# Ten pairs of the mixer's input columns (attention and gate strips) as seven half-size block products each, with their weight sums made in the first FFN

## The chip, the cores and the metric

The kernel runs on one core of one Trainium2 chip. The metric is device time in microseconds (us), as the median of several executions. Five engines work beside each other, each in its own program order: TensorE (PE: matmuls), VectorE (DVE: elementwise), ScalarE (ACT: copies and functions), GpSimd (POOL), and SyncE (SP), which here issues nearly all DMA transfers. An instruction that waits holds up everything behind it on its engine.

## What is computed

One layer of a decoder on 1024 tokens with a model width of 1024. `norm` is a root-mean-square norm with a gain; the two FFNs, the mixer and its three branches are all float32.

```python
f1 = swiglu(norm(h), ffn1_w_in, ffn1_w_out)          # width 2816
h  = h + 0.5 * norm(f1)
u  = norm(h)
p_rwkv, p_swa, q_mem, gate_logits = split(u @ w_in)  # 1792 + 768 + 512 + 3072 columns
y_a = rwkv7_mix(p_rwkv, ...)                         # a recurrence over the 1024 tokens, 8 heads of 64
y_b = sliding_window_gqa_sinks(p_swa, ...)           # 8 query heads, 2 key heads, window 128
y_c = memory_cross_attention(q_mem, mem_n, mem_w_kv) # 4 heads, 256 memory tokens
g_a, g_b, g_c = split(sigmoid(gate_logits + gate_b))
merged = g_a * (y_a @ w_branch[0]) + g_b * (y_b @ w_branch[1]) + g_c * (y_c @ w_branch[2])
h  = h + norm(merged @ w_out)
f2 = swiglu(norm(h), ffn2_w_in, ffn2_w_out)
h  = h + 0.5 * norm(f2)
```

The change touches how part of `u @ w_in` is computed. `w_in` has 6144 columns, held as 48 strips of 128 columns: strips 0 to 13 feed the recurrence, 14 to 19 the window attention, 20 to 23 the memory attention, 24 to 47 the 24 gates (gate g is strip 24 + g).

## The kernel before

**Layout.** Everything stands feature by token: a tile has 128 features as partitions and 512 tokens (`TH`), so the 1024 tokens are two halves, h = 0 and 1, and the model width is eight blocks k. A product of float32 precision is made of three matmuls (`mm3`, L361; lines 364, 365, 366): every factor x is split into a rounded part hi (ACT copies it) and the rest lo (DVE subtracts), and hi·hi, hi·lo and lo·hi are summed in PSUM. One strip of 128 output columns for both halves of the tokens (`project`, L368) is thus 8 x 2 x 3 = 48 matmuls of 128x512.

**Weights.** `plan` (L238) writes down the order in which all weights are used. A raw half strip of 128x512 is loaded by SP into one of five `w_raw` buffers (`raw`, L274, issue at L279), and `operand` (L284) makes `w_hi` on ACT (L288) and `w_lo` on DVE (L290). Eight operands are kept ahead of their use (`OPS`). `take` hands out the next one.

**Block products.** The FFNs already use a scheme with seven half-size products in place of eight: the two strips and the two halves of the tokens are the 2 x 2 blocks of a product, four sums of weight blocks and four of activation blocks ("forms" t1 to t4) are made first, seven products of 4 x 3 = 12 matmuls each follow (84 in place of 96 for two strips), and their results are added on DVE. In the first FFN a pair j of strips runs so, 22 in all (`ffn_in_pair`, L700). While the pairs 9 to 19 run, DVE also makes weight sums for the FFN's second matrix (`sums_loads`, L637, `sums_made`, L650): per step four loads of 128x512 by SP (L641), four DVE operations (L655 to L658), four stores (L660).

**The mixer** (`mixer`, L1584). `rwkv_prep` makes the recurrence's inputs, with DVE nearly full. `rwkv_invert` (L1120) inverts 128 triangular 64x64 matrices on DVE alone: 62 steps of two operations (L1129, L1130), each on the result of the one before, `x` being loaded from `ab_d` (L1124) and stored to `inv_d` (L1132). Meanwhile PE runs the attention strips (`att_block`, tile `pq`) and the first 8 gates (`gate_block`, `GATES_FIRST`, tile `pgate`). Then comes `rwkv_chain` (L1135): 16 steps, each a series of small matmuls on PE and small operations on DVE, ACT and POOL that wait for each other. The scheduler lays the matmuls of the gates 8 and 9 (up to `GATES_EARLY`) into the holes of the chain. After it, `rwkv_finish` and the two attentions run as blocks of 128 tokens: 8 memory blocks, then 8 window blocks (`attention`, L1501). Between a block's scores, its softmax on DVE and ACT, its transposes (`mptr`, `ptr`) and its values, `fill` (L1342) puts a number of other matmuls on PE, given by the list of lumps. These fills come from `filling` (L1317): gates 10 to 23, then the branch products. Each finished gate or branch strip also starts one step of the weight sums for the second FFN (`unit`, L670; tile `gin`, L655).

**Order.** A scheduler orders every engine's queue from program order and priorities; some engines' orders are fixed by `issue_after` and `high_priority`. SP's queue is one: a store that waits for its data stands in the way of the loads behind it.

**PSUM** has eight banks: four for tiles of the large products (`po px py pr pgate pq pb pw`), four for all others.

Of the kernel before, what the change touches and what calls it, by code (L numbers as in the profile page):

```python
# [47 lines left out]
GATES_EARLY = 10  # L48
LUMPS = (30, 54)
GATES_FIRST = 8  # L50
# [173 lines left out]
class Builder:  # L224
# [3 lines left out]

    def out_strip(self, f, n, q):
        a = OUT_FORMS[n][1]  # L230
        return self.sum_d[f][SUMS.index(a), q] if a in SUMS else self.io[f + "_out"][a, q]
# [6 lines left out]
    def plan(self):  # L238
        io, seq = self.io, []
        for f in ("ffn1", "ffn2"):  # L240
# [3 lines left out]
            if f == "ffn1":  # L244
# [4 lines left out]
                seq += [("win", j) for j in ATT_BLOCKS]  # L249
                seq += [("win", 24 + g) for g in range(24)]  # L250
# [386 lines left out]
    def sums_loads(self, f, q, a):  # L637

        with self.tc.issue_after(self.loaded.ins):
            for n, t in enumerate(a):  # L640
                self.nc.sync.dma_start(t, self.io[f + "_out"][n, q])  # L641
        return a

    def sums_tiles(self, pool):
        return [pool.tile([P, KH, P], F32, tag="ws", name="ws", bufs=4) for _ in range(4)]
# [4 lines left out]
    def sums_made(self, f, q, a, behind):  # L650
# [8 lines left out]
        for n, t in zip(SUMS, (a22, a11, a21, a12)):  # L659
            nc.sync.dma_start(self.sum_d[f][SUMS.index(n), q], t)  # L660
# [474 lines left out]
    def rwkv_chain(self, pool, pk_d, inv_d, y):  # L1135
# [65 lines left out]
        n = load(0)  # L1201
        G.memset(n["sv"][lo, 0], 0.0)
# [40 lines left out]
        return lambda: out(NC_ - 1, before)  # L1243

    def rwkv_finish(self, pool, y, bonus_d, ya_d):
# [42 lines left out]
        for i, (p, cols) in enumerate(halves):  # L1288
# [11 lines left out]
            if i % 2:  # L1300
                self.fill(10, end)

# [281 lines left out]
    def mixer(self, u, cp, close_raws, att_d, gate_d, km_d, vm_d):  # L1584
# [7 lines left out]
        self.sg = cp.tile([P, T], F32, name="sg")  # L1592
        with tc.tile_pool(reuse_waits="tile", name="prep", bufs=8) as pool:
            self.rwkv_prep(u, pool, pk_d, ab_d, bonus_d, att_d)
        close_raws()
        with tc.tile_pool(reuse_waits="tile", name="gates", bufs=2) as gp:
            with tc.tile_pool(reuse_waits="tile", name="inv", bufs=1) as pool:
                self.rwkv_invert(pool, ab_d, inv_d)
            for f in ATT_BLOCKS[ATT_FIRST:]:
                self.att_block(f, u, att_d, lambda: gp.tile([P, T], F32, tag="gate", name="att", bufs=2))  # L1600
            for g in range(GATES_FIRST):
                self.gate_block(g, u, gp, gate_d)
            with tc.tile_pool(reuse_waits="tile", name="chain", bufs=2) as pool:
                y = pool.tile([P, NPAIR, T], F32, name="y", bufs=1)
                last = self.rwkv_chain(pool, pk_d, inv_d, y)
                for g in range(GATES_FIRST, GATES_EARLY):
# [6 lines left out]
            with tc.tile_pool(reuse_waits="tile", name="att", bufs=1) as ap, tc.tile_pool(name="attw", bufs=2) as pool:  # L1613
# [54 lines left out]
                self.attention(blocks, [42, 34] + [LUMPS[0]] * (nb - 2) + [LUMPS[1]] * nb, {0: [tables], 1: [keys], 2: [load_values], 4: [turn_values]})  # L1668
# [46 lines left out]
    def build(self):  # L1715
        nc, tc, io = self.nc, self.tc, self.io
        with contextlib.ExitStack() as outer, tc.tile_pool(reuse_waits="tile", name="consts", bufs=1) as cp, \
             tc.tile_pool(reuse_waits="tile", name="w", bufs=1) as self.wpool, \
             tc.tile_pool(reuse_waits="tile", name="pmm", bufs=8, space=bass.MemoryType.PSUM) as self.pmm:
            self.sum_d = {f: tc.dram_tile([len(SUMS), KP, P, KH, P], F32, name=f + "_sum_d") for f in ("ffn1", "ffn2")}  # L1720
            self.plan()
# [25 lines left out]
            form_d = tc.dram_tile([len(OUT_FORMS), KP, P, TH], F32, name="form_d")  # L1747
            first_d = tc.dram_tile([max(FIRST.values()), 2, P, TH], F32, name="first_d")
# [127 lines left out]
```

## Time and profile before

| what | us |
|---|---|
| three executions | 2263.18, 2260.92, 2261.9 |
| median | 2261.9 |
| profiled execution, first to last instruction (span) | 2260.2 |
| PE busy, 11876 matmul instructions | 2236.6 |
| DVE busy, 2719 instructions | 1652.0 |
| ACT busy, 1880 instructions | 1000.2 |
| POOL busy, 114 instructions | 58.1 |

The profiled execution has no time of its own beside its span; the span lies 1.7 us below the median. "Busy" counts the time in which an engine executes something. The stages, in us from the start of the span: the pairs of the first FFN with the weight sums run to about 430, its second matrix and the norms to about 720, `rwkv_prep` to about 900, the inverse from 908 to 1029, the chain from 1048 to about 1150, the attentions from about 1180 to about 1450. Rows called "windows" give, for a stretch A:B, its length, then each engine's busy time with its count of instructions (PE, PE's weight loads, DVE, ACT, POOL), the granted PE clock, the share of time in which the 16 DMA engines were busy, and what they moved in GB/s.

### The profile page before, as it was taken

How to read it: one execution, taken by the hardware profiler on the slowest of the kernel's cores; microseconds unless marked ns; L12 is line 12 of the kernel's file. 1: busy time of each engine (PE TensorE's matmuls, PEld its weight loads, DVE VectorE, ACT ScalarE, POOL GpSimd, SP SyncE). 2: the span in 40 equal slices, each digit the busy share in tenths (PEclk: the TensorE clock that was granted, in tenths of full speed). 3: DMA queues.
4: the chain of work that ended last, by engine and by line, in shares of the span. 5: the costliest groups of instructions: out<-in, count | busy, mean ns of one | idle time of the engine just before them, and what ended most of it. 6: DMA issues, size and time to landing. Idle time of an engine off the chain costs nothing.

```text
span 2260.2 us, 33447 instructions
## 1 busy us (share of the span) xinstructions
PE 2236.6 (99%) x11876; PEld 1840.4 (81%) x11876; DVE 1652.0 (73%) x2719; ACT 1000.2 (44%) x1880; POOL 58.1 (3%) x114
## 2 busy tenths in 40 slices
PE   8999999999999999999999999999999999999998
PEld 6888888888888788888888887788888888888887
DVE  6987777666698886995666576684898885656576
ACT  6533333454556653223454445334663233345451
POOL 0000000000000000001320000000000000000000
PEclk9999999999999999999999999999999999999999
DMA  8465666686654467325438885654565542347663
GB/s 291 157 210 168 215 212 208 214 276 207 191 173 149 117 143 183 118 93 194 144 113 289 266 278 186 209 177 136 173 214 188 189 168 90 116 165 250 204 196 122
DMA packets 280775, 417.66 MB, mean 185 GB/s; under 512 B 82304, under 2 KB 104320, under 8 KB 280352
## 3 DMA queue, kind: packets, MB, share of 16 engines
q1 hardware_dynamic: 272832, 400.26, 55.3%
q10 hardware_dynamic: 7776, 15.28, 2.0%
q8 instruction: 93, 1.52, 0.3%
q14 instruction: 74, 0.61, 0.1%
HBM read 284.89 MB, written 129.50 MB: 183 GB/s over the span
## 4 chain that ended last, share of the span: by engine, by line
PE 93%; DVE 4%; DMA 1%; ACT 1%; issue 1%; SPq 0%; DVEq 0%; ACTq 0%
PE px L365 7%; PE px L364 7%; PE px L366 7%; PE po L365 6%; PE po L366 6%; PE po L364 6%; PE pgate L364 4%; PE pgate L366 4%; PE pgate L365 4%; PE pz L365 3%; PE pz L364 3%; PE pz L366 3%; PE pb L364 2%; PE pb L365 2%; PE pb L366 2%; PE pr L364 2%
## 5 line engine op out<-in xcount | busy, mean ns | idle before, releaser
L288 ACT CAST w_hi<-w_raw 128x512 fp32r<-128x512 f32 x594 | 367.5, 620 | 734.5 <-PE px L365 159.7
L290 DVE TENSOR_TENSOR w_lo<-w_raw,w_hi 128x512 fp32r<-128x512 f32 x594 | 407.6, 687 | 196.0 <-ACT w_hi L288 175.2
L366 PE MATMUL po<-u,w_lo 128*128 128x512 f32 (+1 forms) x476 | 180.9, 380 | 0.0
L364 PE MATMUL po<-u,w_hi 128*128 128x512 f32 (+1 forms) x476 | 180.9, 380 | 0.0
L365 PE MATMUL po<-u,w_hi 128*128 128x512 f32 (+1 forms) x476 | 180.9, 380 | 0.0
L364 PE MATMUL pgate<-u,w_hi 128*128 128x512 f32 x384 | 153.2, 399 | 0.0
L366 PE MATMUL pgate<-u,w_lo 128*128 128x512 f32 x384 | 151.4, 394 | 0.0
L365 PE MATMUL pgate<-u,w_hi 128*128 128x512 f32 x384 | 149.8, 390 | 0.0
L365 PE MATMUL px<-f,w_hi 128*128 128x512 f32 x352 | 137.2, 390 | 1.0 <-DVE f L473 1.0
L364 PE MATMUL px<-u,w_hi 128*128 128x512 f32 x352 | 137.0, 389 | 0.8 <-DVE km L1442 0.8
L364 PE MATMUL px<-f,w_hi 128*128 128x512 f32 x352 | 137.1, 389 | 0.1
L366 PE MATMUL px<-u,w_lo 128*128 128x512 f32 x352 | 137.0, 389 | 0.0
L366 PE MATMUL px<-f,w_lo 128*128 128x512 f32 x352 | 137.0, 389 | 0.0
L365 PE MATMUL pz<-u,w_hi 128*128 128x512 f32 x352 | 137.0, 389 | 0.0
L365 PE MATMUL px<-u,w_hi 128*128 128x512 f32 x352 | 136.9, 389 | 0.0
L364 PE MATMUL pz<-u,w_hi 128*128 128x512 f32 x352 | 136.9, 389 | 0.0
L366 PE MATMUL pz<-u,w_lo 128*128 128x512 f32 x352 | 136.9, 389 | 0.0
L473 DVE TENSOR_TENSOR u<-hid,u 128x512 fp32r<-128x512 f32 x114 | 78.3, 690 | 46.5 <-ACT u L472 43.5
L364 PEld LDWEIGHTS po<-u,w_hi 128*128 128x128 f32 x476 | 89.5, 188 | 17.1
L365 PEld LDWEIGHTS po<-u,w_hi 128*128 128x128 f32 x476 | 89.5, 188 | 17.1
L366 PEld LDWEIGHTS po<-u,w_lo 128*128 128x128 f32 x476 | 89.5, 188 | 16.8
L472 ACT CAST u<-hid 128x512 fp32r<-128x512 f32 x114 | 70.7, 620 | 64.3 <-DMA hid<-form_d 55.7
(401 smaller groups left out, 5097.4 us busy)
## 6 DMA issues: line engine op xcount, KB each, us to landing
w_raw<-in_ffn_in SPq DMA_DIRECT2D x220, 256.0 KB
hid<-form_d SPq DMA_DIRECT2D x154, 256.0 KB
w_raw<-in_win SPq DMA_DIRECT2D x112, 256.0 KB
form_d<-g SPq DMA_DIRECT2D x88, 256.0 KB
w_raw<-ffn_sum_d SPq DMA_DIRECT2D x88, 256.0 KB
form_d<-h SPq DMA_DIRECT2D x66, 256.0 KB
w_raw<-in_ffn_out SPq DMA_DIRECT2D x66, 256.0 KB
gate_d<-gate SPq DMA_DIRECT2D x24, 512.0 KB
```

The source lines that it names most:

```text
L288: self.nc.scalar.copy(hi, x)
L290: self.split_last = self.nc.vector.tensor_tensor(lo, x, hi.bitcast(F32), ALU.subtract)
L364: mm(out, wh, xh, start=first, stop=False, **kw)
L365: mm(out, wh, xl, start=False, stop=False, **kw)
L366: self.last_mm = mm(out, wl, xh, start=False, stop=last, **kw)
L472: self.nc.scalar.copy(hi, x)
L473: self.nc.vector.tensor_tensor(lo, x, hi.bitcast(F32), ALU.subtract)
```

## The change

Ten pairs of strips are computed with the seven products: the three attention pairs (16, 17), (20, 21), (22, 23) and the seven pairs of the gates 0 to 13. Their weight sums (four for each pair) are made during the first FFN: a second set of four DVE operations, four loads and four stores stands beside the set already there in the steps j = 9 to 16, and the pairs 8 and 9 of the ten have theirs in j = 20 and 21. The sums go to `win_sum_d` and come back as weights. `pre_norm` now writes the normed activations in place and stores them to `xn_d`; `mix_forms` loads them in pieces (`part`, five buffers), makes the four sums per k and splits them. `win_pair` runs the seven products and three DVE additions. The second halves of strips 14 and 15 and gate 14 come first, then the ten pairs beside `rwkv_invert`; the chain has the gates 15 and 16 beside it, and `filling` the gates 17 to 23, so the lumps between the attention blocks are smaller.

```diff
-GATES_EARLY = 10
-LUMPS = (30, 54)
-GATES_FIRST = 8
+GATES_EARLY = 17
+LUMPS = (18, 36)
+GATES_FIRST = 14
+ATT_PAIRS = ((16, 17), (20, 21), (22, 23))
+WIN_PAIRS = ATT_PAIRS + tuple((24 + g, 25 + g) for g in range(0, GATES_FIRST, 2))
+SECOND_UNITS = 8
...
@@ plan
-                seq += [("win", j) for j in ATT_BLOCKS]
-                seq += [("win", 24 + g) for g in range(24)]
+                seq += [("win", j) for j in FILL]
+                seq += [("win", 24 + GATES_FIRST)]
+                seq += [("win_out", (i, n)) for i in range(len(WIN_PAIRS)) for n in range(7)]
+                seq += [("win", 24 + g) for g in range(GATES_FIRST + 1, 24)]
...
@@ pre_norm
-            t = pool.tile([P, TH], F32, tag="un", name="un", bufs=2)[:, : hi - lo]
-            self.nc.vector.scalar_tensor_tensor(t, xs[k], self.vec(gname, k), rs, ALU.mult, ALU.mult)
-            self.split(t, *(y[:, lo:hi] for y in u[k][h]))
+            self.nc.vector.scalar_tensor_tensor(xs[k], xs[k], self.vec(gname, k), rs, ALU.mult, ALU.mult)
+            self.split(xs[k], *(y[:, lo:hi] for y in u[k][h]))
+            self.nc.sync.dma_start(self.xn_d[:, k, h * TH + lo : h * TH + hi], xs[k])
...
@@ ffn_in
-                if f == "ffn1" and FIRST[f] <= j < FIRST[f] + KP:
-                    self.sums_made(f, j - FIRST[f], self.sums_loads(f, j - FIRST[f], self.sums_tiles(pool)), made)
+                if f == "ffn1" and j >= FIRST[f]:
+                    i = j - FIRST[f]
+                    if i < SECOND_UNITS:
+                        self.sums_made("win", i, self.sums_loads("win", i, self.sums_tiles(pool, f"sq{TH}")), self.up)
+                    what = (f, i) if i < KP else ("win", i - KP + SECOND_UNITS)
+                    if what[0] == f or what[1] < len(WIN_PAIRS):
+                        self.sums_made(*what, self.sums_loads(*what, self.sums_tiles(pool)), made)
...
+    def mix_forms(self, u, pool, parts):
...
+        with self.tc.high_priority(offset=self.lead):
+            for k in range(KH):
+                x12, x22, x11, x21 = (parts() for _ in range(4))
+                for t, j, h in ((x12, k, 1), (x22, k + KH, 1), (x11, k, 0), (x21, k + KH, 0)):
+                    self.nc.sync.dma_start(t, self.xn_d[:, j, h * TH : (h + 1) * TH])
+                V.tensor_tensor(x22, x22, x12, ALU.subtract)
+                V.tensor_tensor(x12, x12, x11, ALU.subtract)
+                V.tensor_tensor(x11, x22, x11, ALU.add)
+                V.tensor_tensor(x21, x21, x11, ALU.subtract)
+                for n, x in (("t2", x11), ("t1", x12), ("t3", x22), ("t4", x21)):
+                    self.split(x, *fs[n][k])
+        return fs
+
+    def win_pair(self, i, fs, parts, out, att_d, gate_d):
...
+        part(0, "b11", px, True)
+        x = kept(px)
+        part(1, "b21", py, True, True)
+        made(0, first, 0, py, x)
+        part(2, "t2", px)
+        u1 = kept(px)
+        part(3, "t1", pz, True)
+        z = kept(pz)
+        part(4, "t3", px)
+        made(1, second, 1, px, z)
+        part(5, "b22", pz, False, True)
+        made(0, first, 1, pz, u1)
+        part(6, "t4", px, False, True)
+        made(1, second, 0, px)
...
@@ mixer
-                self.rwkv_invert(pool, ab_d, inv_d)
-            for f in ATT_BLOCKS[ATT_FIRST:]:
-                self.att_block(f, u, att_d, lambda: gp.tile([P, T], F32, tag="gate", name="att", bufs=2))
-            for g in range(GATES_FIRST):
-                self.gate_block(g, u, gp, gate_d)
+                fs = self.mix_forms(u, forms, parts)
+                for f in FILL[ATT_FIRST:]:
+                    self.att_block(f, u, att_d, out)
+                self.gate_block(GATES_FIRST, u, gp, gate_d)
+                self.rwkv_invert(pool, ab_d, inv_d)
+                for i in range(len(WIN_PAIRS)):
+                    self.win_pair(i, fs, parts, out, att_d, gate_d)
...
-                self.attention(blocks, [42, 34] + [LUMPS[0]] * (nb - 2) + [LUMPS[1]] * nb, {0: [tables], 1: [keys], 2: [load_values], 4: [turn_values]})
+                self.attention(blocks, [26, 20] + [LUMPS[0]] * (nb - 2) + [LUMPS[1]] * nb, {0: [tables], 1: [keys], 2: [load_values], 3: [turn_values]})
```

**Where it moves instructions.** On DVE, at the start of the inverse (`itmp<-inv` and `inv<-inv,itmp` are its two operations per step), there stood before:

```order
L290 TENSOR_TENSOR w_lo<-w_raw,w_hi 128x512 x7
L1129 TENSOR_TENSOR itmp<-inv 128x62
L1130 TENSOR_TENSOR inv<-inv,itmp 128x62
L1129 TENSOR_TENSOR itmp<-inv 128x122
L1130 TENSOR_TENSOR inv<-inv,itmp 128x2x61
L1129 TENSOR_TENSOR itmp<-inv 128x180
L1130 TENSOR_TENSOR inv<-inv,itmp 128x3x60
```

At the same place in the changed kernel, the sums of the activation blocks (`part<-part`) and their splits (`mix_form`) for k = 1 stand between the first steps; those for k = 2 and 3 follow in the same way:

```order
L1147 TENSOR_TENSOR itmp<-inv 128x62
L302 TENSOR_TENSOR w_lo<-w_raw,w_hi 128x512
L1148 TENSOR_TENSOR inv<-inv,itmp 128x62
L1336 TENSOR_TENSOR part<-part 128x512
L302 TENSOR_TENSOR w_lo<-w_raw,w_hi 128x512
L1337 TENSOR_TENSOR part<-part 128x512
L1147 TENSOR_TENSOR itmp<-inv 128x122
L1338 TENSOR_TENSOR part<-part 128x512
L1148 TENSOR_TENSOR inv<-inv,itmp 128x2x61
L1339 TENSOR_TENSOR part<-part 128x512
L302 TENSOR_TENSOR w_lo<-w_raw,w_hi 128x512
L485 TENSOR_TENSOR mix_form<-part,mix_form 128x512
```

So 24 operations on the forms for k = 1 to 3 share DVE with the inverse's first steps. On SP, at the same place, the changed kernel has the loads of those pieces behind the inverse's load and, for k = 2, behind a store of gate 14:

```order
L1142 DMA inv<-ab_d 128x4096
L1335 DMA part<-xn_d 128x512 x4
L291 DMA w_raw<-win_sum_d 128x512 x2
L291 DMA w_raw<-in_win 128x512
L1401 DMA gate_d<-gate 128x1024
L291 DMA w_raw<-in_win 128x512
L1335 DMA part<-xn_d 128x512 x4
```

Before, only loads of weights and stores of attention strips stood behind `inv<-ab_d`. On PE, near the end of the chain, one step read before as follows (`z`, `y`, `gram`, `bkt` are the chain's, `pgate` the gate products laid in):

```order
L1145 MATMUL gram<-f 128x128 x8
L1145 MATMUL z<-uv,bk 64x64 x8
L1187 MATMUL bkt<-ident,f 128x128 x4
L366 MATMUL pgate<-u,w_lo 128x512
L364 MATMUL pgate<-u,w_hi 128x512
L365 MATMUL pgate<-u,w_hi 128x512
L366 MATMUL pgate<-u,w_lo 128x512
L364 MATMUL pgate<-u,w_hi 128x512
L365 MATMUL pgate<-u,w_hi 128x512
L1145 MATMUL z<-sv,gz 64x64 x8
```

In the changed kernel this holds for the first steps, while in the last ones it reads:

```order
L1163 MATMUL gram<-f 128x128 x8
L1163 MATMUL z<-uv,bk 64x64 x8
L1205 MATMUL bkt<-ident,f 128x128 x4
L1163 MATMUL z<-sv,gz 64x64 x8
L1163 MATMUL y<-gz,uv 64x64 x8
```

Before, six of the 96 matmuls of the gates 8 and 9 stood in each step. Of the 96 of the gates 15 and 16, 29 now stand ahead of the chain, so that step 11 (of 16) has two left and the four steps after it have none.

More of the change, by code (lines that the diff above doesn't have):

```diff
@@ L1301, in rwkv_finish @@
                 self.fill(10, end)
+    def mix_forms(self, u, pool, parts):
+        V = self.nc.vector
+        tile = lambda: pool.tile([P, TH], F32R, tag="mix_form", name="mix_form", bufs=8 * KH)
+        fs = {"b11": [u[k][0] for k in range(KH)]}
+        for n, h in (("b21", 0), ("b22", 1)):
+            fs[n] = [u[k][h] for k in range(KH, KD)]
+        for n in ("t2", "t1", "t3", "t4"):
+            fs[n] = [(tile(), tile()) for _ in range(KH)]
+        with self.tc.high_priority(offset=self.lead):
[10 more added lines that the diff above has]
+        return fs
@@ L1592, in mixer @@
         self.sg = cp.tile([P, T], F32, name="sg")
+        over = contextlib.ExitStack()
+        beside = over.enter_context(tc.tile_pool(reuse_waits="tile", name="mix_parts", bufs=5, side="right"))
+        parts = lambda: beside.tile([P, TH], F32, tag="part", name="part")
         with tc.tile_pool(reuse_waits="tile", name="prep", bufs=8) as pool:
```

59 lines of the change are left out of this document (47 added, 12 removed).

## The prediction

> **What bounds the kernel now.** I read the page's busy shares first, then its chain of work that ended last.
>
> ```profile
> span 2260.2 us, 33447 instructions
> ...
> PE 2236.6 (99%) x11876; PEld 1840.4 (81%) x11876; DVE 1652.0 (73%) x2719; ACT 1000.2 (44%) x1880; POOL 58.1 (3%) x114
> ...
> PE 93%; DVE 4%; DMA 1%; ACT 1%; issue 1%; SPq 0%; DVEq 0%; ACTq 0%
> ```
>
> TensorE is busy for 99% and holds 93% of the chain. So matmuls that go are worth their full pace, and a new wait of PE costs its full length. Over the whole span other engines have room; what decides is the room at the places where the change adds work. I read those as windows: first the pairs of the first FFN and what follows them, then the inverse, then the attentions.
>
> ```profile
> 250.00:300.00 50.00, 50.00 (x222) 41.40 (x222) 36.64 (x60) 19.08 (x33) 0.00 (x0) 1.00 0.66 217
> ...
> 250.00:425.00 175.00, 175.00 (x773) 144.95 (x773) 126.42 (x205) 65.04 (x111) 0.20 (x1) 1.00 0.63 211
> 425.00:480.00 55.00, 54.89 (x242) 45.13 (x241) 36.62 (x71) 26.31 (x47) 2.60 (x14) 1.00 0.80 267
> ...
> 461.00:480.00 19.00, 19.00 (x85) 15.73 (x84) 11.83 (x32) 7.58 (x14) 0.25 (x4) 1.00 0.96 326
> ...
> 760.00:800.00 40.00, 39.00 (x285) 31.41 (x283) 38.01 (x42) 25.97 (x41) 0.32 (x3) 1.00 0.57 135
> ...
> 910.00:960.00 50.00, 50.00 (x222) 41.41 (x221) 48.59 (x60) 9.51 (x17) 0.00 (x0) 1.00 0.27 93
> ```
>
> The reader is to see three things. PE runs 222 matmuls of 128x512 in 50 us, so one costs 50/222 = 0.2252 us, with forms (250 to 300) and with strips (910 to 960) alike. DVE has a quarter free in the FFN's pairs, next to nothing in `rwkv_prep` (38.01 of 40) and beside the inverse (48.59 of 50). DMA stands at 0.63 in the pairs and 0.80 just behind them.
>
> **The change part by part.** *Matmuls.* Ten pairs at 84 in place of 96 remove 120: 120 x 0.2252 = **-27.0 us**, if PE then never waits more than it did.
>
> *First FFN.* A second set of sums adds four DVE operations and eight transfers of 256 KB to each of eight pairs, and two sets to later steps.
>
> ```profile
> 404.31 0.69 DVE L290 TENSOR_TENSOR w_lo<-w_raw,w_hi 128x512 fp32r<-128x512 f32 x1
> 404.91 0.68 DVE L655 TENSOR_TENSOR ws<-ws 128x512 f32<-128x512 f32 x1
> ...
> 385.00:404.00 19.00, 19.00 (x86) 15.73 (x85) 14.69 (x25) 7.08 (x12) 0.20 (x1) 1.00 0.71 246
> ...
> 10.00:15.00 5.00, 5.00 (x24) 4.39 (x24) 3.79 (x6) 3.77 (x7) 0.00 (x0) 1.00 1.05 396
> ...
> 1242.10:1259.20 17.10, 15.52 (x84) 13.07 (x83) 7.38 (x18) 7.04 (x23) 0.00 (x0) 1.00 0.93 303
> ...
> DVE w_sum L315 <- DMA w_raw<-in_ffn_in: 3.8, 5, 1.0
> ```
>
> DVE operations of this size start 0.60 us apart when they follow each other. A pair lasts 84 x 0.2252 = 18.9 us; 4 x 0.60 = 2.4 us more makes the fuller of two such windows 17.1 of 19. That fits. The transfers add 2.1 MB per 18.9 us, 111 GB/s, to 211: 322 GB/s, or by share 0.63 x 322/211 = 0.96. In the two late steps it is the stretch at 0.80 that gets 4.2 MB more. The trace holds such a load without harm (461 to 480: 326 GB/s, PE full; at the start even 396), and with harm (1242 to 1259: 303 GB/s, PE 1.58 us short). Eight pairs at 1.58 make the upper bound 12.6, the lower is 0. The nearest row is 461 to 480, loads of the same kind and size from the same queue, so I stay low; but `w_sum` already waits for its loads five times, and SP has eight more issues per pair in front of some loads. I take **+3**.
>
> [...]
>
> *Norm and prep.* 16 stores of `xn_d` and, ahead of the inverse, the four sums and four splits for k = 0. They lie where DVE has 2 of 40 us free and PE already is 1.00 us short (760 to 800). Eight operations at 0.60 are 4.8 us if nothing hid them; part of `rwkv_prep` has PE full. I take **+1**, between 0 and 4.8.
>
> *Forms for k = 1 to 3.* These DVE operations were not there before. The activation sums start when the inverse's load lands, since a step of the inverse stands ahead of them in DVE's queue.
>
> ```profile
> 906.87 0.59 ACT L1496 COPY att<-pq 128x512 f32<-128x512 f32 x1
> ...
> 908.36 0.22 DVE L1129 TENSOR_TENSOR itmp<-inv 128x62 f32<-128x62 f32 x1 [0.67 <-DMA inv<-ab_d]
> ...
> 1024.81 0.52 DVE L1130 TENSOR_TENSOR inv<-inv,itmp 128x342 f32<-128x342 f32 x1
> ```
>
> Strip 16, 48 matmuls, ended at about 906.7 (its copy follows at 906.87); gate 14 with its 48 takes that place. From there PE has 83 matmuls, 18.7 us, that need no form of k = 3: until 925.4. On DVE, from 908.4 on, stand 24 form operations, 6 `w_lo` and an addition (31 x 0.60 = 18.6) and 17 operations of the inverse from 0.22 us upward (one of 342 elements takes 0.52), together about 6: the last form of k = 3 comes at about 933, the t1 among it at 931. PE stands some 6 us, in several pieces. The load of the pieces for k = 2 also stands behind gate 14's store on SP and needs freed buffers. Bounds: 2, if the loads come early and PE reaches the form later; 12, if each of three rounds of loads adds 2 us. I take **+6**.
>
> *The pairs beside the inverse.* 53.2 us for each of the inverse's two lines:
>
> ```profile
> 860.00:1060.00 200.00, 53.21 (x62) 1.00 0.46 147
> ...
> 860.00:1060.00 200.00, 53.25 (x62) 1.00 0.46 147
> ```
>
> A pair gives DVE 7 `w_lo` and 3 additions, 6.0 us. The inverse, 106.5 us, stretches in DVE's queue over nearly nine pairs, 12.3 each: 18.3 us against PE's 18.9. That is even; I take **0**, with 3 as the other end. The inverse ends with more than a pair of matmuls ahead of the chain, so its store and load stay covered.
>
> *Chain.* In a step PE waits for DVE, and the gate matmuls fill that wait.
>
> ```profile
> 1103.21 0.69 PE L1145 MATMUL z<-sv,gz 128*64 128x64 f32 x16
> ...
> 1107.83 0.65 PE L1187 MATMUL bkt<-ident,f 128*128 128x128 f32 x4
> ...
> 1108.23 0.48 PE L366 MATMUL pgate<-u,w_lo 128*128 128x512 f32 x1
> ...
> 1108.72 0.86 DVE L1239 TENSOR_TENSOR sv<-ts,sw 64x256 f32<-64x256 f32 x2
> ...
> 1109.81 0.57 PE L1145 MATMUL z<-sv,gz 128*64 128x64 f32 x12
> ```
>
> A step takes 1109.81 - 1103.21 = 6.60 us. The next `z` can't start before `sv` ends at 1109.58, and from 1108.23 to there six gate matmuls (1.35 us) fill PE. They don't set the step's length. Step 11 now has 2 of 6 and the four after it none: 28 matmuls, 28 x 0.2252 = **+6.3 us**, run elsewhere at full price while the step stays as long. Lower bound 3.5, if a step without `w_lo` on DVE (0.68 us in the step) is about 0.6 us shorter in five steps.
>
> *Attentions.* The lumps shrink by a third or more.
>
> ```profile
> DVE gin L655 <- DMA gin<-in_ffn_out: 13.7, 4, 6.6
> ...
> PE msc L94 <- DVE gin L655: 1.6, 1, 1.6
> ...
> 1396.00:1413.00 17.00, 17.00 (x94) 13.37 (x93) 10.09 (x23) 8.00 (x27) 0.00 (x0) 1.00 0.25 80
> 1413.00:1430.00 17.00, 17.00 (x94) 13.26 (x93) 10.76 (x29) 7.77 (x28) 0.00 (x0) 1.00 0.28 94
> ```
>
> A window block of 17 us has 54 fills, 12.2 us; with 36 it has 13.0. DVE's 10.1 to 10.8 fits, but steps of the FFN's sums (4 x 0.60) that now fall here bring some blocks to 13. In the memory blocks DVE stood four times for the loads of `gin`, 13.7 us in all, and PE lost only 1.6 since 30 fills covered the rest. With 18 fills that cover is 12 x 0.2252 = 2.7 us shorter. I take 2.7 for the longest of these waits and 1.3 for window blocks, **+4**; bounds 0, and 13.7 if all four waits came through.
>
> Sum: -27.0 + 3 + 1 + 6 + 0 + 6.3 + 4 = **-6.7** on the span of 2260.2: 2253.5. The median of the runs shown, 2261.9, lies 1.7 above the span: **2255 us**. With every cost at its lower bound it is -27 + 2 + 3.5 = -21.5, 2240; with every one at its upper bound (12.6, 4.8, 12, 3, 6.5, 13.7) it would be +25.6, 2288.
>
> **The rivals.**
>
> *Nearly all of it arrives*: the scheduler's order reads worse than it runs, the forms come in time, and chain and blocks absorb the rest. Time between the full -27.0 and the lower bounds: 2235 to 2245, about 2240. For it: PE is short by under 2 us at all its single waits after the first load. Against it: the order of the chain's last steps is fixed, and so is the forms' work on DVE.
>
> *Slower: memory traffic in the first FFN becomes the bound.* It decides from the point where the queue grants less than 322 GB/s in the steps 9 to 16. At the 303 of the harmed row a pair takes 18.9 x 322/303 = 20.1 us, 1.2 more, 9.5 in eight; and the 14.7 MB of 425 to 480 plus 4.2 need 62.4 us in place of 55, another 7.4. That is 17 in place of 3: 2255 + 14 = 2269. For it: 0.96 leaves nothing for the uneven pairs (246 GB/s in one). Against it: 326 and 396 were reached, and eight operands ahead, 8 x 12 x 0.2252 = 21.6 us, carry PE over a late load.
>
> *The attentions run dry*: all four `gin` waits come through, 13.7 in place of 4: 2265, no change. For it: DVE at over 90% in 13 us. Against it: the waits fell in memory blocks alone.
>
> *DVE behind PE beside the inverse*: forms at 12, pairs at 3, prep at 2: +10, 2265.
>
> *Gaps slow PE's clock.* A gap of the forms' length could lower the granted clock and make the following matmuls dearer. At half pace for as long as the gap, 6 us, it would cost 3 more: 2258.
>
> ```profile
> PE pq L1355 <- DMA mkv<-in_mkv_k: 6.5, 1, 6.5
> ...
> 0.00:10.00 10.00, 3.53 (x9) 2.92 (x10) 1.60 (x8) 6.05 (x11) 0.70 (x6) 1.00 0.81 304
> ```
>
> The one gap of that size in this trace, 6.5 us at the start, leaves the clock at 1.00, so I give it little. [...]
>
> **How the numbers follow.** Chances: the forecast 0.46 (2247 to 2262; 0.36 of it faster, 0.10 within), nearly all of it 0.17 (faster), memory traffic 0.14 (0.02 within, 0.12 slower), attentions 0.12 (0.06 and 0.06), DVE 0.08 (0.04 and 0.04), the clock 0.03 (0.01 faster, 0.01 within, 0.01 slower). 0.2%, 4.5 us, is about what a measurement of this kernel can tell from no change: below 2257.4 is faster, above 2266.4 slower. That makes 0.54, 0.23 and 0.23. The range goes from 2240, all costs at their lower bounds, to 2274, past the price of the slower rival.
>
> **What would show it.** The gain: 120 fewer matmuls of 128x512, and still 222 of them in 50 us. Forms: PE waiting for `mix_form` some 10 to 30 us after the inverse's load, 6 us in all. Chain: steps 12 to 15 with 1 to 1.4 us of PE idle before `z`, step time still 6.6. First FFN: pairs of 18.9 us with a DMA share near 0.96; pairs over 20 us would mean the slower rival. Attentions: window blocks of 13 us; memory blocks in which PE waits behind `gin`. Wrong would be a chain whose steps shorten without their fills, or PE waits in the FFN's pairs above 10 us.

## The result: 0.8% slower

| kernel | median, us | runs | ratio to before, 95% interval |
|---|---|---|---|
| before | 2262.54 | 4 | |
| changed | 2280.06 | 4 | 1.0077 [1.0063, 1.0091] |

Forecast was 2255 with a range to 2274: the change cost 17.5 us where about 7 were to be gained. The page of the changed kernel, its busy shares, clock and chain:

```profile
span 2279.2 us, 33765 instructions
...
PE 2230.2 (98%) x11756; PEld 1827.1 (80%) x11756; DVE 1723.1 (76%) x2851; ACT 1039.1 (46%) x1947; POOL 58.7 (3%) x114
...
PE 80%; DVE 8%; DMA 7%; issue 2%; ACT 2%; SPq 1%; DVEq 0%; POOL 0%; ACTq 0%
```

The 120 matmuls are gone, yet PE is busy only 6.4 us less, where 27 were to go; PE's share of the chain (the work that ended last, followed back) fell from 93% to 80%. To find the place, I cut both traces at the first or last matmul of a tile and took from each stage the number of its 128x512 matmuls times 0.2252 us. What is left holds waits, small matmuls and slow pace; its difference is what the change cost there.

| stage (ends with) | ends before, us | ends after, us | cost of the change | forecast |
|---|---|---|---|---|
| first FFN, gates and pairs (first `po`) | 459.7 | 465.1 | +5.4 | +3 for this and the next |
| its second matrix, norms (first `pr`) | 670.4 | 679.5 | +3.8 | |
| `rwkv_prep` and the strips behind it (first `pgate`) | 960.7 | 904.0 | -1.0 | +1 |
| beside the inverse (first `z`) | 1050.7 | 1127.1 | +13.1 | +6 forms, 0 pairs |
| chain (last `z<-sv,gz`) | 1150.0 | 1225.6 | +5.5 | +6.3 |
| `rwkv_finish` (first `msc`) | 1203.6 | 1279.0 | 0.0 | |
| memory blocks (first `sc`) | 1299.1 | 1351.9 | +1.7 | +4 for this and the next |
| window blocks (last `ptr`) | 1433.9 | 1472.9 | +17.3 | |
| rest | 2260.2 | 2279.2 | +0.4 | |

Sum +46.2, less 27.0: +19.2 against 19.0 of the spans. The forecast was -6.7 on the span, so the miss is 25.7, and the window blocks alone are two thirds of it. 0.2252 is slightly low: matmuls start 0.2267 us apart in both kernels (221 starts in the 50 us from 250 on before; the 222 of the prediction count those that the window's edges cut). With 0.2267 the stage beside the inverse costs 12.3 and `rwkv_prep` -0.6; the others move by 0.2 or less.

A stage cost also differs from profile to profile. Over the profiles below whose edit doesn't touch the stage, the pairs of the first FFN cost 3.9 to 7.9, its second matrix 2.9 to 5.4, the window blocks 17.1 to 19.5. A difference of 2 us in one of these three is thus not resolved.

PE's waits in the changed kernel, behind that for the first load, which it had before too (6.0 here, 6.5 there):

```profile
PE z L1163 <- DVE sv L1258: 5.6, 5, 1.3
PE mpv L97 <- DVE sc L131: 4.0, 1, 4.0
PE msc L97 <- DVE gin L673: 3.7, 1, 3.7
PE px L376 <- ACT u L738: 3.6, 5, 1.0
PE sc L97 <- DVE pt L165: 1.9, 2, 1.7
PE po L376 <- ACT u L484: 1.8, 1, 1.8
```

The columns are us in total, times, longest. The first is the chain's empty steps. The second is in the window blocks. Its origin, in the timeline of that place:

```profile
1363.40 0.40 ACT L149 ACTIVATE sc<-sc,st 128x128 f32<-128x128 f32 x1 [2.95 <-DMA ffn_sum_d<-gin]
...
1364.85 0.69 DVE L673 TENSOR_TENSOR gin<-gin 128x512 f32<-128x512 f32 x1 [4.42 <-DMA gin<-in_ffn_out]
...
1368.07 0.69 DVE L1657 SCALAR_TENSOR_TENSOR u<-gin,pb 128x512 f32<-128x512 f32 x1 [2.53 <-DMA gin<-gate_d]
...
1370.51 0.80 PE L97 MATMUL mpv<-mpt,vm_in 128*128 128x128 f32 x2 [3.99 <-DVE sc L131]
```

DVE stood 4.42 us for the weights of a sum of the second FFN (`gin`), then 2.53 for a gate's load, and the softmax stood behind both. ACT's softmax stood 2.95 us behind a gate load that it issues itself and that needed a buffer which a sum's store still held. Before the change 7 of the 11 steps of these sums began ahead of the first window scores and 4 behind them (the expectation of one trial below says 8 and 3); now it is 3 and 8, of which seven lie in the window blocks and one behind them. A sum's step is started by a finished gate or branch strip, and of the twelve gates that started them five are left.

The windows show what such waits did to the clock:

```profile
481.00:485.30 4.30, 2.52 (x11) 1.67 (x10) 0.69 (x1) 0.99 (x2) 0.00 (x0) 1.00 1.05 393
485.30:488.70 3.40, 3.40 (x9) 2.67 (x8) 2.40 (x4) 3.33 (x7) 0.00 (x0) 0.50 1.03 316
929.00:932.40 3.40, 1.31 (x5) 0.60 (x4) 3.40 (x8) 2.18 (x4) 0.00 (x0) 1.00 0.34 90
932.40:939.20 6.80, 5.87 (x14) 4.11 (x13) 6.80 (x14) 2.25 (x4) 0.00 (x0) 0.50 0.35 110
939.20:946.00 6.80, 6.77 (x29) 5.19 (x28) 6.35 (x12) 3.74 (x7) 0.00 (x0) 1.00 0.28 77
1369.30:1376.10 6.80, 5.59 (x25) 5.59 (x26) 6.80 (x22) 1.71 (x4) 0.00 (x0) 0.50 0.54 166
1423.90:1430.70 6.80, 6.80 (x18) 4.96 (x17) 6.73 (x20) 2.85 (x7) 0.00 (x0) 0.50 0.81 274
```

Four times between 10 and 2270 us the granted clock is 0.50, for 3.4 or 6.8 us, 23.9 us in all, each time with a wait of PE just ahead. From 932.4 on 14 matmuls run in 6.8 us, and right behind it 29. So each of these waits cost its own length and up to half of what the halved clock lasted, 12 us in all. Two of the four stretches lie in the window blocks: up to 6.8 of their 17.3 us are the clock. Before the change no window between 10 and 2250 us was below 1.00.

The trace records these four stretches with 3.413 us (the first) and 6.827 us (the other three). Their starts, 485.26, 932.40, 1369.31 and 1423.92, lie 131.0, 259.0 and 275.0 times 3.413 us apart from the first, so in this run they stand on one grid.

The length of a wait alone doesn't decide: one of 1.78 us was enough at 484, and one of 3.7 us at 1316 was not. In the steps of that grid just ahead of the four stretches PE stood, as the profile counts idle time, for 1.78, 2.09, 2.79 and 1.67 us of the 3.413. Of the other steps at full clock between 12 and 2219 us, the two that share the wait at 1316 have most, 1.76 and 1.94 us, and no other has more than 1.26. So the grid splits the longer wait, while the one at 484 fell into one step. But 1.67 us was enough in one place and 1.94 us not in another: a value that decides isn't shown.

### The profile page after: what moved, and what is told of

Its sections match the earlier page's. It is cut to its first block, busy times and chain, and to the rows that moved or that the text cites. A ratio compares the mean times of both kernels' runs of the same rounds, so it can differ in the third digit from the quotient of the medians.

```text
span 2279.2 us, 33765 instructions
## 1 busy us (share of the span) xinstructions
PE 2230.2 (98%) x11756; PEld 1827.1 (80%) x11756; DVE 1723.1 (76%) x2851; ACT 1039.1 (46%) x1947; POOL 58.7 (3%) x114
## 4 chain that ended last, share of the span: by engine, by line
PE 80%; DVE 8%; DMA 7%; issue 2%; ACT 2%; SPq 1%; DVEq 0%; POOL 0%; ACTq 0%
PE px L376 8%; PE px L378 8%; PE px L377 8%; PE po L376 6%; PE po L377 6%; PE po L378 6%; PE pz L376 4%; PE pz L377 4%; PE pz L378 4%; PE pr L376 2%; PE pr L377 2%; PE pr L378 2%; DVE w_lo L302 1%; PE pw L376 1%; PE pw L378 1%
## 5 line engine op out<-in xcount | busy, mean ns | idle before, releaser
L300 ACT CAST w_hi<-w_raw 128x512 fp32r<-128x512 f32 x624 | 386.3, 620 | 726.8 <-PE px L377 187.0
L302 DVE TENSOR_TENSOR w_lo<-w_raw,w_hi 128x512 fp32r<-128x512 f32 x624 | 428.5, 688 | 164.0 <-ACT w_hi L300 148.4
L376 PE MATMUL px<-u,w_hi 128*128 128x512 f32 x392 | 152.6, 389 | 0.8 <-DVE km L1528 0.8
L377 PE MATMUL px<-u,w_hi 128*128 128x512 f32 x392 | 152.6, 389 | 0.0
L378 PE MATMUL px<-u,w_lo 128*128 128x512 f32 x392 | 152.6, 389 | 0.0
L377 PE MATMUL pz<-u,w_hi 128*128 128x512 f32 x392 | 152.6, 389 | 0.0
L376 PE MATMUL pz<-u,w_hi 128*128 128x512 f32 x392 | 152.5, 389 | 0.0
L378 PE MATMUL pz<-u,w_lo 128*128 128x512 f32 x392 | 152.5, 389 | 0.0
L377 PEld LDWEIGHTS po<-u,w_hi 128*128 128x128 f32 x476 | 90.0, 189 | 17.1 <-DVE u L485 0.2
L376 PE MATMUL pr<-u,w_hi 128*128 128x512 f32 x224 | 87.7, 393 | 0.0
L377 PE MATMUL pr<-u,w_hi 128*128 128x512 f32 x224 | 87.2, 390 | 0.2 <-DVE u L485 0.2
L376 PEld LDWEIGHTS px<-u,w_hi 128*128 128x128 f32 x392 | 73.6, 188 | 17.0 <-ACT r L484 1.6
```

The costliest lines, as they stand in the source:

```text
L300: self.nc.scalar.copy(hi, x)
L302: self.split_last = self.nc.vector.tensor_tensor(lo, x, hi.bitcast(F32), ALU.subtract)
L376: mm(out, wh, xh, start=first, stop=False, **kw)
L377: mm(out, wh, xl, start=False, stop=False, **kw)
L378: self.last_mm = mm(out, wl, xh, start=False, stop=last, **kw)
```

## The experiments

Stage costs are read as in the table above; the changed kernel is meant where no other is named. The runs were measured in five rounds, each with the kernel before beside them; its median lay between 2262.5 and 2264.1, so that differences under 2 us between medians of two rounds say little.

**Where the window blocks' 17 us come from.** Three trials on the changed kernel.

```diff
-                self.units = self.sums_beside()
+                self.units = iter(())
...
+        if f == "ffn2" and a in SUMS:
+            return self.io[f + "_out"][SUMS.index(a), q]
```

> The changed kernel without the second FFN's weight sums that run beside the attention blocks (11 steps of four loads, four DVE operations and four stores); the second FFN's second matrix takes plain strips in place of its sums, so that its output is another. Theory A: the window blocks of the changed kernel lose 17 us because those steps, now in the window blocks, make DVE and the buffers they share with the gate loads stand for transfers; without them the stretch from the first window scores to the last ptr falls by 14 to 17 us and the kernel to 2263 to 2267. Theory B: the lumps of 36 matmuls are too short for the softmax between them whatever else runs; then it falls by no more than 4 us, to 2276 or so.

Measured 2261.32 (8 runs), 18.7 less than the changed kernel and a little below the range of theory A. The window blocks fell by 16.9, to before's own level (+0.4), the memory blocks by 3.6; no halved clock is left there. The window rows of the blocks, first before the change, then of the changed kernel, then without the sums:

```profile
1279.00:1434.00 155.00, 155.00 (x858) 124.17 (x857) 108.19 (x264) 79.86 (x255) 0.00 (x0) 1.00 0.66 216
```

```profile
1326.00:1473.00 147.00, 138.66 (x759) 109.62 (x757) 120.89 (x291) 77.46 (x257) 0.00 (x0) 0.95 0.78 253
```

```profile
1326.00:1455.00 129.00, 128.97 (x752) 102.54 (x751) 103.58 (x261) 76.82 (x258) 0.00 (x0) 1.00 0.53 165
```

With the same lumps of 36 PE now is full: without the sums the lumps are long enough for the softmax. So the sums beside the blocks are the cause of the 17 us, and theory B alone doesn't hold. Through which of DVE's waits, the shared buffers and the gate loads they act, this run doesn't say.

```diff
-LUMPS = (18, 36)
+LUMPS = (18, 44)
```

> The changed kernel with lumps of 44 in place of 36 in the eight window blocks: 64 matmuls (14.5 us) come from behind the last block into the blocks; nothing is left out. Theory B (lumps too short): 12 us less, 2268. Theory A (DVE and ACT stand for the sums' transfers): the waits that are set by transfers stay, 2276 to 2280, and what is gained in the blocks may be lost behind them where 64 matmuls are missing.

Measured 2281.18. The window blocks got 2.0 better, memory blocks and tail 2.4 worse. Lumps of 44 don't pay with the sums in place, and theory B falls. The 54 of before weren't tried, so what the shorter cover adds where a sum's step falls into a block stays open.

```diff
-        nc, V = self.nc, self.nc.vector
+        nc, V = self.nc, self.nc.gpsimd if f == "ffn2" else self.nc.vector
```

> The changed kernel with the second FFN's weight sums beside the attentions made on GpSimd in place of DVE; nothing is left out. Theory A, first half (DVE's own queue stands for the loads): 6 to 14 us less, 2266 to 2274. [...]

Measured 2298.34: worse by 18, not better; the window blocks cost 24.3. GpSimd needs about 1.35 us for one (39.05 us busy with 29 operations from 1330 to 1485); its eight operations of this size in the changed kernel (`ysq`) take 1.04 to 1.49 us, so the 1.0 of the expectation was their shortest. SP stands 28.3 us in these 155 us until GpSimd has made what SP is to store, and DVE now stands 8.7 us once for a gate's load. So it isn't enough to take the sums off DVE's queue: what waits for the shared buffers and for SP remains. With a slower engine in the place of DVE the run can't tell what each of them costs.

**Another place for these sums, ahead of the attentions.** `sums_early` (its body isn't shown) yields between the loads of a step and its four sums, for five steps.

```diff
+        early = self.sums_early(pool, EARLY)
+        next(early)
         self.fill(22, self.behind)
...
                 self.fill(8 if p < NPAIR - 1 else 30, end)
+                next(early, None)
```

> The changed kernel with five of the eleven steps of the second FFN's weight sums made beside rwkv_finish, before the attentions, in tiles that the chain no longer needs; nothing is left out. Then 3 steps stand in the memory blocks and 3 in the first window blocks, as before the change 8 and 3. Theory A: the window blocks lose 10 to 16 of their 17 us, 2264 to 2270, and the halved clock there goes. Rival: the steps cost the same beside rwkv_finish, where DVE works on PE's inputs too: 2276 to 2282.

Measured 2302.19. The window blocks gained 9.3, but `rwkv_finish` lost 24.3 and the memory blocks 7.2: there DVE makes what PE waits for next. The rival's ground holds, at a price 20 us above its range. With nine of the eleven steps now ahead of the first window scores the window blocks still cost 8.0, so the number of steps that fall into them isn't all of it.

**The first FFN.**

```diff
-            return (a1, a2, *(self.win_sum_d[n, m] for m in (1, 0, 2, 3)), b2)[q]
+            return (a1, a2, *self.win_halves((n + 1) % len(WIN_PAIRS)), b2)[q]
...
-                    if i < SECOND_UNITS:
-                        self.sums_made("win", i, self.sums_loads("win", i, self.sums_tiles(pool, f"sq{TH}")), self.up)
```

> The changed kernel without the weight sums of the ten pairs in the first FFN (40 DVE operations, 40 loads, 40 stores fewer); the pairs take plain strips as weights, so that their output is another. Theory C: these sums cost the first FFN 9 us up to the start of the recurrence's strips (5.4 in the pairs by late weights, 3.7 behind them, half of that by the clock): the kernel falls to about 2271, and the start of the strips from 679.5 to about 670.5. Rival: the loss is from the stores and the in-place norm; then it stays at 2278 to 2280.

The strips of the recurrence start at 671.6, 7.9 us earlier: the sums' price in the first FFN, with the pairs at +1.2 and the second matrix at +0.1 against before. That is theory C. The kernel's time fell only to 2278.3 (2275.1 to 2279.6), which is the rival's range: in this profile the memory blocks came out 1.1 and the window blocks 1.9 worse, and their waits move from run to run.

How the sums do it shows at 300 us in the changed kernel, where PE waits 0.90 us for an accumulator to be copied:

```profile
296.54 0.69 DVE L673 TENSOR_TENSOR ws<-ws 128x512 f32<-128x512 f32 x1 [0.31 <-DMA ws<-in_win]
297.26 0.69 DVE L674 TENSOR_TENSOR ws<-ws 128x512 f32<-128x512 f32 x1
297.87 0.68 DVE L714 TENSOR_TENSOR g<-py,m 128x512 f32<-128x512 f32 x1
```

```profile
298.59 0.63 ACT L715 ACTIVATE g<-g 128x512 f32<-128x512 f32 x1 [3.58 <-DVE g L714]
299.13 0.60 ACT L300 CAST w_hi<-w_sum 128x512 fp32r<-128x512 f32 x1
299.64 0.58 ACT L738 COPY u<-px 128x512 f32<-128x512 f32 x1
```

Two sums stand ahead of the addition on DVE; the activation on ACT waits for that, and the copy that frees PE's accumulator stands behind the activation. But DVE was late already, since it stood for weight loads. From 291 to 391 us, first before the change, then changed:

```profile
DVE w_sum L315 <- DMA w_raw<-in_ffn_in: 1.3, 2, 0.7
```

```profile
DVE w_sum L327 <- DMA w_raw<-in_ffn_in: 16.8, 6, 3.2
```

The loads for which `w_sum` stood took 3.1 to 3.5 us from issue to landing before (246 to 402 us), 4.6 to 6.2 us in the changed kernel (265 to 409). So slower transfers and the order in the queues act together, and no run here separates them.

```diff
-SECOND_UNITS = 8
+SECOND = (4, 5, 6, 7, 8, 9, 11, 13, 15, 17)
```

`SECOND` lists the steps of the first FFN in which the sums of the ten pairs are made.

> The changed kernel with the ten pairs' weight sums made in the first FFN's steps 4 to 8 and in the odd ones from 9 to 17, in place of 9 to 16, 20 and 21; nothing is left out. Theory C (late weights where two sets of sums meet in one step, and two sets at the start of the second matrix): the five waits of the pairs 13 to 17 and the wait with the halved clock behind them go, the recurrence's strips start at 671 to 673 in place of 679.5, the kernel falls by 6 to 8 to about 2273. Rival: it is the sum of bytes in the first FFN, wherever they stand; then 2278 to 2281.

Measured 2282.86, above both expectations; the strips start at 677.0, 2.5 earlier: the second matrix lost its 3.8, the pairs cost 1.2 more. Half of theory C held. The rest was lost to the window blocks' waits (+2.2) and others.

**The forms, the clock, the pace.** `split_made` is the last split of `mix_forms`.

```diff
-                self.rwkv_invert(pool, ab_d, inv_d)
+                with tc.issue_after(self.split_made.ins):
+                    self.rwkv_invert(pool, ab_d, inv_d)
```

> The changed kernel with the inverse's first step behind the last form in DVE's queue; nothing is left out. Theory: PE's waits for the forms (4.2 us, and 3 more through the clock halved from 932.4 on) come from the 17 operations of the inverse between them and from waiting for its load; without them 5 to 7 us less, 2274, and no halved clock near 932. The inverse, 10 to 15 us later, still ends before the pairs do. Rival: the loads of the pieces set the forms' pace (five buffers): 0 to 2 less.

The stage beside the inverse fell by 3.7 and no halved clock is left near 932; the kernel measured 2279.23, as the window blocks took 2.1 back. The size is under the expectation, and its ground doesn't hold: PE's idle time for forms and pieces there is 2.9 us in place of 3.2. What went is the halved clock, about 3 us, and 1.4 of the wait for the chain's first load. It didn't come again: in the three versions below that have this edit but not the chain's, the stage costs 12.9 to 13.4, with 1.7 to 1.9 us for the chain's load and a clock that is halved once or twice.

```diff
                 self.gate_block(GATES_FIRST, u, gp, gate_d)
+                idle = self.psum("idle")
+                for _ in range(18):
+                    nc.tensor.matmul(idle, u[0][0][0][:, :P], u[0][0][0], start=True, stop=True)
```

> The changed kernel with 18 matmuls of 128x512 more, whose results nothing reads, between gate 14 and the first pair (18 x 0.2252 = 4.1 us of PE work more); the outputs are unchanged. If the halved clock near 932 follows from PE standing for the forms, the waits of 4.2 us there shrink to under 1 and the clock stays whole: the stretch from the first gate matmul to the chain gets 0 to 4 us shorter although PE does 4.1 us more. If the waits are set by something that moves along with PE, it gets 4.1 longer.

The stage took 222.2 us (904.0 to 1126.2) in place of 223.1 (904.0 to 1127.1), with 18 matmuls more. The waits for forms shrank to 0.2 us or less each and the clock stayed whole at the place of the halved one:

```profile
932.40:939.20 6.80, 6.57 (x27) 4.46 (x26) 6.33 (x12) 3.48 (x7) 0.00 (x0) 1.00 0.41 128
```

27 matmuls in place of 14. Of the forms' price about 3 us is thus the clock, 4.2 the waits (from start to start of the matmuls; 3.2 of it is idle time). The kernel as a whole measured 2284.38 (2281.5 to 2287.3), its profiled execution 2279.7.

```diff
-            with tc.tile_pool(reuse_waits="tile", name="inv", bufs=1) as pool, \
-                 tc.tile_pool(reuse_waits="tile", name="mix_forms", bufs=1) as forms:
+            with tc.tile_pool(reuse_waits="tile", name="mix_forms", bufs=1) as forms, \
+                 tc.tile_pool(reuse_waits="tile", name="inv", bufs=1) as pool:
```

> The changed kernel with the forms' tiles allocated ahead of the inverse's, so that they lie 20 KB lower in each partition; nothing is left out. In the pairs, matmuls that read a form start 0.233 us apart, others 0.227. If the place of the tile in memory decides, the pace of these matmuls changes (to 0.227) or moves to others; if it is what reads or writes beside them, it stays 0.233.

The matmuls that read a form still start 0.233 us apart (424 of them; one execution, 2282.99), so this shift of place doesn't decide. What does is open.

**The chain.** `G` is GpSimd, `begun` the last matmul ahead of the first `z`.

```diff
-            nc.sync.dma_start(n["f"], pk_d[c])
+            queue = nc.sync if c else G
+            queue.dma_start(n["f"], pk_d[c])
...
+                with tc.issue_after(self.begun.ins):
                     for g in range(GATES_FIRST + 1, GATES_EARLY):
```

> The changed kernel with the chain's first load issued by GpSimd in place of SP, where it stood behind the last pair's stores, and with the gates 15 and 16 held back until the chain has begun, so that none of their matmuls stands ahead of it and each step has six again; nothing is left out. Theory: the chain starts where the pairs end (1116 in place of 1124) with six fills in every step: 1.7 us of the load's wait and the 5.5 of the four empty steps go, 7 us less, 2273. Rival: the chain's empty steps are shorter by what the fills took; then no more than 2 less.

Measured 2283.4 (2278.5 to 2287.8). Inconclusive on the whole: the second load, still on SP behind the stores, came 3.3 us late, the first step took 12.4 us, and the clock was halved. But the steps behind it took 6.59 us with six fills, against 6.51 for an empty one in the changed kernel: the fills are nearly free, so an empty step wastes them.

**Versions that put it together.** First the second FFN's sums in that FFN's own steps from `SUMS2` = 11 on.

```diff
-                self.units = self.sums_beside()
...
+                if f == "ffn2" and 0 <= j - SUMS2 < KP:
+                    self.sums_made(f, j - SUMS2, self.sums_loads(f, j - SUMS2, self.sums_tiles(pool, f"sq{TH}")), made)
```

> The changed kernel with the second FFN's weight sums taken from beside the attentions and made in that FFN's own steps 11 to 21, on DVE, in tiles of its norm; nothing is left out. Before the change DVE is busy for 30 to 32 of 50 us there and DMA for 0.28 to 0.36. Theory A: the attention stages fall as they did without the sums (17 us in the window blocks, 3 to 4 in the memory blocks), the second FFN takes no more time: 2260 to 2264. Rival: these steps cost the second FFN what two sets cost the first (5 to 8 us): 2266 to 2270.

The same edit on the kernel before the change:

> The kernel before the change with the second FFN's sums in that FFN's own steps 11 to 21; nothing is left out. Its attention blocks had 30 and 54 matmuls between them, and PE lost 1.6 us there in all: 0 to 2 us less than before, 2261 to 2263. If it gains more than 5, the sums were a cost before the change too, and the moved sums are no part of what the change lacked.

With the edit "forms first" from above added:

> The kernel with the second FFN's sums in its own steps, and in addition the inverse's first step behind the last form; nothing is left out. The gains of the two should add: 3.7 less than with the sums moved alone, 2256 to 2261. If the forms' gain is only passed on to the next wait (the inverse ends later, the chain's load with it), 0 to 1 less.

With `SECOND` from above added:

> The kernel with the second FFN's sums in its own steps and the forms first, and in addition the ten pairs' sums in the first FFN's steps 4 to 8 and the odd ones 9 to 17; nothing is left out. The two sets at the start of the second matrix cost 3.8, which should go, while the pairs cost 1 more: 2 to 3 less than without this edit, 2253 to 2259.

```diff
-SUMS2 = 11
+SUMS2 = 8
```

> As the kernel with moved sums, forms first and spread sums, but with the second FFN's sums in that FFN's steps 8 to 18 in place of 11 to 21; nothing is left out. With 11 to 21, PE stood 2.6 us for a form at about 2051 and 1 us at 2075, and the clock was halved for 3.4 us behind it; if that comes from the last sets meeting the loads for the second matrix, as in the first FFN, it goes: 3 to 4 less, 2256. If the sums cost this FFN their transfers wherever they stand, no change, 2260.

With the chain's edit added, now for two loads:

```diff
-            queue = nc.sync if c else G
+            queue = G if c < 2 else nc.sync
```

> The same, and in addition the chain's first two loads issued by GpSimd and the gates 15 and 16 held back until the chain has begun; nothing is left out. In the earlier trial the first load came in time and the 14 later steps took 6.59 with six fills, but the second load, still on SP behind the stores, came 3.3 us late, the first step took 12.4 in place of 6.1 and the clock was halved. With both loads off SP: 1.7 + 5.9 = 7.6 less than without this edit, about 2249. If GpSimd's loads come late as well, no gain.

| kernel | median, us | ratio to before, 95% interval |
|---|---|---|
| changed, sums moved to steps 11 to 21 | 2263.61 | 1.0001 [0.9992, 1.0010] |
| before, sums moved likewise | 2267.35 | 1.0015 [1.0005, 1.0024] |
| + forms first | 2262.81 | 0.9995 [0.9985, 1.0006] |
| + pairs' sums spread | 2259.88 | 0.9987 [0.9977, 0.9996] |
| + sums in steps 8 to 18 | 2259.0 | 0.9980 [0.9971, 0.9989] |
| + chain's loads and fills | 2255.25 | 0.9966 [0.9954, 0.9979] |

Moving the sums gives back 16.4 us; the window blocks stand at before's level (+0.4). Nothing is left out there, and the stage readings agree with the run without the sums (memory blocks -2.1). The move costs the second FFN up to 5 (PE stood 2.6 us at 2051, then a halved clock); with the steps 8 to 18 the part behind the attentions came to 1.0 over before, though the median fell by 0.9 and not by the expected 3 to 4. Before the change the same move loses 3.6: its window blocks don't gain (0.0), as there the sums' waits were covered. "Forms first" gave 0.8 on the median, less than its interval. In the last one the steps of the chain are 6.58 with six fills and the chain costs nothing against before (-0.3, with 93 fills inside as there); 3.8 of the expected 7.6 arrived. PE's longest waits there:

```profile
PE px L377 <- DVE att L1370: 2.4, 1, 2.4
PE px L377 <- ACT mix_form L485: 2.2, 1, 2.2
```

The second was there without the edit too (2.0). The first is new: it stands ahead of the last product of the pairs, with the clock halved behind it, and the stage beside the inverse came out 2.1 dearer. This version beats both kernels, by 7.6 us and by 24.8.

## Why the prediction was wrong, step by step

- *Matmuls, -27.0*: right; 120 fewer, at 0.2267 each (27.2; the working's 0.2252 counts matmuls that the window cuts).
- *Attentions, +4*: 19.0. **This is the step that failed.** I counted what DVE does in a window block (10 to 11 us, plus 2.4 for a sum's step) against 13 us, and priced only a shorter cover for the four waits in the memory blocks. The bound of 13.7 was those waits' old length. But the gates taken away were also what started the sums early; with them gone, seven of eleven steps (before: four) went into the window blocks, with transfers, shared buffers and gate loads in the softmax's queues, and two halved clocks behind the waits. Without the sums these blocks cost 0.4 in place of 17.3, and with the sums moved into the second FFN likewise; lumps of 44 don't help. How much of the 17 is the later start, the shorter cover, the buffers or the clock isn't separated.
- *Gaps slow PE's clock*, a chance of 0.03: this rival came true, and I had all but ruled it out. It happened four times, up to 12 us. My evidence against it was the first window's 1.00 behind a wait of 6.5 us. But that same row has 9 matmuls in 3.53 busy us, and the next 24 in 5.00: the pace spoke against the clock column, and I read the column alone. The granted clock is recorded from 9.6 us on. The filler run shows the price directly.
- *First FFN, +3*: 9.2 with what follows it. I took the row of 326 GB/s to mean that such a load does no harm. In the eight pairs that load for both sets 301 GB/s were moved on the mean (47.4 MB in the 157.5 us from 233.9 to 391.4), close to the 303 that the slower rival assumed, and the weight loads landed late (above). So its mechanism did occur, in part: the pairs cost 5.4 where it had 9.5, since the pairs 10 to 12 ran full at 298 to 340 GB/s, and what follows 3.8 where it had 7.4. The pairs 13 to 17, and then 11 and 12:

```profile
291.10:390.40 99.30, 95.68 (x417) 77.58 (x416) 77.84 (x127) 33.99 (x60) 0.00 (x0) 1.00 0.89 295
252.90:291.10 38.20, 38.20 (x171) 31.61 (x170) 30.21 (x49) 13.85 (x25) 0.00 (x0) 1.00 0.92 306
```

- *Forms, +6*: about 7.3, waits 4.2 and clock 3. Right in place; that the size is near is partly luck, as the clock was not in my sum.
- *Pairs, 0*: DVE kept up, but 3 us went to a pace of 0.233 in 480 matmuls, and 1.7 to the chain's first load, which stood on SP behind the last pair's stores; I had called that load covered. With the forms that is 12.0 of the 12.3 of this stage.
- *Chain, +6.3*: 5.5; steps of 6.51 without fills, 6.59 with. Right, and the lower bound's reason (a shorter step) is worth 0.08 a step. (Five steps of 0.6 less also make that bound 3.3, not 3.5.)
- *Norm and prep, +1*: -1.0 (-0.6 at 0.2267), so the stores and forms there cost nothing that this table shows.

The range ended at 2274 since no rival had two costs high at once: the attentions' and the clock's belong together, as each of the four stretches at 0.50 had a wait of PE just ahead.

## What to carry to other kernels

Work taken off the bound engine also takes away cover and triggers: list what was hidden under each removed piece and what its end started, and ask where that goes. Read room on an engine by what stands ahead of what in its queue and by when its loads land, not by its busy share. Price a new wait of the matmul engine above its own length, as the clock here was at 0.50 for 3.4 or 6.8 us behind four of them.

## What the runs showed of the hardware

- In the changed kernel the granted clock was 0.50 for 3.413 us once and for 6.827 us three times, with all four starts on a grid of 3.413 us. PE had stood for 1.67 to 2.79 us of the step ahead of each; two steps with 1.76 and 1.94 us had no halving behind them. Matmuls started 0.427 us apart there, in place of 0.227.
- In the pairs, matmuls reading a form start 0.233 us apart, those of the first, second and sixth product 0.228, 0.227 and 0.228. Neither DVE's inverse (0.2333 us up to its end at 1086.2, 0.2332 behind it) nor a place 20 KB lower changes it; the cause stays open.
- A 128x512 sum takes about 1.35 us on GpSimd, as the profile counts it, beside a DVE busy for 122.5 of 155 us, against 0.69 on DVE.
